# Queries and keys of two strided attention groups by seven half-size products each

## The chip, the cores and the metric

The kernel runs on one core of one Trainium2 chip. The metric is the time of one execution on the device in microseconds (us); the time before is the median of 3 runs.

## The reference

A decoder trunk of two layers over 512 tokens of width 1024, in float32. The first layer mixes tokens by dilated attention, the second by a gated recurrence; each is followed by a convolutional feed-forward network (FFN). The change lies in the attention: 24 heads of width 128 in three groups of eight, with dilations 1, 4 and 16, whose outputs are mixed by their softmax denominators. All queries, keys and values come from one product:

```python
def dilated_attention_mixer(x, w_qkv, w_o, rel_bias):
    qkv = (x @ w_qkv).reshape(B, S, N_GROUPS, 3, HEADS_PER_GROUP, HEAD_DIM)
    for g in range(N_GROUPS):
        o, lse = dilated_group_attention(qkv[:, :, g, 0], qkv[:, :, g, 1], qkv[:, :, g, 2],
                                         tbl, WINDOWS[g], DILATIONS[g])
...
    alpha = jax.nn.softmax(jnp.stack(lses), axis=0)
    o = jnp.sum(alpha[..., None] * jnp.stack(outs), axis=0)
    return o.reshape(B, S, ATTN_OUT_WIDTH).astype(x.dtype) @ w_o
```

## The kernel before, in words

**Precision.** Each float32 factor is cut into a high part and the rest (whi and wlo of a weight, ahi and alo of an activation). A product is three matmuls that add up in a PSUM bank: high by high, high by low, low by high (`PASSES`). The high part is a rounding copy on ACT (L253, half pieces L184), the low part a subtraction on DVE (L265, L185) that waits for it.

**Weights.** All weights stream from HBM in an order written out at the end of the kernel: `plan` lists the loads, `splits` the pieces that are cut from them. `load` issues the loads on SP's queue, with two buffers (`raw`). `pump` cuts the next pieces, if their load has landed by the count of steps (`landed`) and fewer than eight pieces are alive (`W_UNITS`); `tick` runs what is scheduled beside, then calls `pump`. `take` hands a piece to the product that needs it, and cuts it there and then if that has not been done. What `pump` has cut gets its low part later, from `low_parts`, which the next cut or `take` calls. So each engine's instructions stand in the order in which this code emits them, and each engine carries them out in that order.

**Tiles.** `feat_tiles` makes two query or key blocks at a time, one for each head of a pair, each a tile of 24 matmuls of 128x512 (L436) into a bank `ps`. A pair of heads has four such tiles for each of the two strided groups (numbers 1 and 2): queries and keys of both heads. `qk_sink` copies a bank to a tile qk, queries with the scale on ACT (L1181), keys on DVE (L1183). `step` follows each two tiles.

**Beside.** The scores of the pair ahead run as side tasks: products S (L1413), a bias and row sums on DVE (L1294), exponentials on ACT (L1401), weights and transposes on DVE (L1460, L1462), and products O (L1492), copied by ACT (L1495) and added on DVE (L1496).

**Seven for eight.** Values of the local and strided groups, and part of the FFN, are made by seven products of quarters of the matrices instead of eight (`product`, L654, for values; `sevenths`, with 24 matmuls of 128x256 each, L874, for the FFN). They need sums of weight quarters. These are made by transfers on POOL's queue: `add_up` issues a plain load (`first`, L309), and behind it loads that add to what stands there (`sum`, L311). The sums live in one buffer, so the next sum's first load is held until the last low part of the one ahead has been cut: a piece's `behind` entry in `after`, looked up in `finished`. Of two sums, a third is made by an addition on DVE (`mix`, L219). The sums of tokens (T, `token_sums`) are made once for the values. A bank that later products add to is copied by ACT (`kept`, L591).

In the FFN a product of `sevenths` is followed by a plain tile, by its `yield`.

Of the kernel before, what the change touches and what calls it, by code (L numbers as in the profile page):

```python
# [18 lines left out]
P = 128  # L19
# [27 lines left out]
DOWN_AT = (3, 5, 6, 7, 8, 9, 12, 13, 15, 16, 17, 18, 19, 22)  # L47
WIDE_STEPS = (1, 3, 1, 2)
# [47 lines left out]
def kernel(  # L96
# [110 lines left out]
    def split_next(i, j):  # L207
        splits.append((i, j))
        todo[i] += 1
# [204 lines left out]
    def w_seven(w, a, b, beside, before):  # L414

        n = len(plan)
        add("first", 4, 256, [(corner_of(w, 0, b), 256)], before.get("mix"), False)
        add("sum", 4, 256, [(corner_of(w, 0, a), 256)], None, False)
        add("first1", 4, 256, [(corner_of(w, 1, b), 256)], before.get("sum"), False)
        v0 = w_cols(w, beside[0], own=False)  # L420
        left = w_cols(w, a, "halves", False)
        mix = add("mix", 4, 256, [], None, False)
        v1 = w_cols(w, beside[1], own=False)
        last = add("last", 8, 256, [(corner_of(w, 1, b), 4), (corner_of(w, 0, b), 4), (corner_of(w, 1, b), 4)], None, False)
        more = add("sum1", 4, 256, [(corner_of(w, 1, a), 256)], (mix, 1), False)
        for key in (
            (v0, 0), (mix, 0), (v0, 1), (left, 0), (left, 1), (mix, 1), (v1, 0), (last, 0), (v1, 1), (last, 1), (more, 0),
        ):
            split_next(*key)
        before.update(mix=(mix, 0), sum=(more, 0))  # L430
# [232 lines left out]

    def two(s="vq"):
        return [psum(s) for _ in range(2)]
# [172 lines left out]
    def ffn(layer, hT, post, pre, spill):  # L838
# [27 lines left out]
        def sevenths(j, n):  # L866
            outs = {}

            def product(bank, piece, act, first=True):
                W = take(*piece)  # L870
                for n in range(2):
                    for k in range(4):
                        for p, (a, b) in enumerate(PASSES):
                            mm(  # L874
                                bank[:, n * 256 : (n + 1) * 256],
                                W[a][:, k, n * P : (n + 1) * P],
                                woven(act(b)[:, k, :]),
                                start=first and (n, k, p) == (0, 0, 0),
                                stop=(k, p) == (3, 2),
                                skip_group_check=True,  # L880
                            )
                done()

# [13 lines left out]
            product(W, (n + 5, 0), total_of(3))  # L897
            w = kept(W, -1.0)
            yield
            product(X, (n + 4, 0), corner(hT, 0, 0))  # L900
# [3 lines left out]
            product(Z, (n + 4, 1), corner(hT, 1, 0))  # L904
            out(0, 0, c, Z, add)
            yield
            product(X, (n + 5, 1), total_of(2), False)
            u = kept(X, -1.0)
            yield
            product(W, (n + 7, 0), total_of(4), False)  # L910
            out(1, 0, u, W, sub)
            yield
            product(X, (n + 7, 1), total_of(1), False)
# [4 lines left out]
            product(Z, (n + 8, 0), corner(hT, 1, 1))  # L918
# [186 lines left out]
    def attention(hT, post, pre, spill):  # L1105
# [57 lines left out]
        def qk(ps, scale, permute, turned=True, halves=False):  # L1163
# [20 lines left out]
            return o  # L1184

# [375 lines left out]
        for hp in range(4):  # L1561
# [4 lines left out]
            for j in range(4):  # L1566
# [9 lines left out]
                feat_tiles(1, hT, lambda m, ps: sink(2 * j + m, ps), between=held if last and j == 3 else None, paired=False)  # L1576
# [177 lines left out]
    for hp in range(4):  # L1754
        if hp == 0:
            w_value(qkv, (2 * D, 512))
        for j in range(2):
            w_cols(qkv, j * D + hp * 256)
            value_part("l", hp, j)
    for hp in range(4):  # L1760
        for c, (g, j) in enumerate(((1, 0), (1, 1), (2, 0), (2, 1))):
            w_cols(qkv, g * 3 * D + j * D + hp * 256)
            value_part("s", hp, c)
    for c in range(4):
        w_rows(attn_w_o[0], c * 256)
# [122 lines left out]
```

## Time and profile before

| | us |
|---|---|
| median of 3 runs | 1373.49 (1370.64 to 1374.04) |
| the profiled execution | 1373.19 |
| its span, first to last instruction | 1371.2 |
| TensorE busy in it | 1352.8 |
| DVE busy | 1026.3 |
| ACT busy | 692.2 |

The mean clock that TensorE was granted is 0.997 of full. The profile's page gives each engine's busy time and share of the span, the groups of instructions by line with their mean duration in ns, and the transfers by queue. A timeline lists single instructions, with the start and the duration in us, the engine, the line, the operation and its tiles; the bracket is the idle time ahead of it and what ended it. The chain of waits goes back from the last instruction, and has for each piece its start, its length and what it was. PE is TensorE, PEld its weight loads.

### The profile page before, as it was taken

How to read it: one execution, taken by the hardware profiler on the slowest of the kernel's cores; microseconds unless marked ns; L12 is line 12 of the kernel's file. 1: busy time of each engine (PE TensorE's matmuls, PEld its weight loads, DVE VectorE, ACT ScalarE, POOL GpSimd, SP SyncE). 2: the span in 40 equal slices, each digit the busy share in tenths (PEclk: the TensorE clock that was granted, in tenths of full speed). 3: DMA queues.
4: the chain of work that ended last, by engine and by line, in shares of the span. 5: the costliest groups of instructions: out<-in, count | busy, mean ns of one | idle time of the engine just before them, and what ended most of it. 6: DMA issues, size and time to landing. Idle time of an engine off the chain costs nothing.

```text
span 1371.2 us, 18713 instructions
## 1 busy us (share of the span) xinstructions
PE 1352.8 (99%) x7109; PEld 1199.5 (87%) x7109; DVE 1026.3 (75%) x1790; ACT 692.2 (50%) x1169; POOL 111.8 (8%) x126
## 2 busy tenths in 40 slices
PE   9999999999999999999999999999999999999997
PEld 6888888888888889998888889888898998888886
DVE  7787573637667679877958769878979877958765
ACT  5434432414355554455645545579655455645642
POOL 2211021011000001000000010000001000000110
PEclk9999999999999999999999999999999999999999
DMA  8979779596748354555668793233144565768771
GB/s 256 246 223 282 189 189 253 197 218 165 237 152 302 107 170 114 157 175 123 200 175 197 203 270 123 93 123 122 62 148 121 163 185 116 207 170 196 210 192 62
DMA packets 184236, 243.10 MB, mean 177 GB/s; under 512 B 16632, under 2 KB 135936, under 8 KB 184146
## 3 DMA queue, kind: packets, MB, share of 16 engines
q1 hardware_dynamic: 151456, 184.82, 41.1%
q0 software_dynamic: 32688, 57.09, 21.7%
q8 instruction: 56, 0.92, 0.3%
q14 instruction: 34, 0.28, 0.1%
q10 hardware_dynamic: 2, 0.00, 0.0%
HBM read 218.23 MB, written 28.36 MB: 180 GB/s over the span
## 4 chain that ended last, share of the span: by engine, by line
PE 60%; DVE 9%; ACT 4%; issue 2%; DMA 1%; POOL 0%; DVEq 0%; ACTq 0%; POOLq 0%
PE ps L436 35%; PE acc L436 8%; PE X L654 5%; PE vq L654 3%; PE W L654 3%; PE X L874 2%; DVE wlo L265 2%; PE Z L874 2%; PE W L874 2%; DVE xb L1607 1%; DMA sum<-in_attn_w_qkv_dram 1%; PE O L1492 1%; DVE x L551 1%; DVE post L546 1%; DVE th L1662 1%
## 5 line engine op out<-in xcount | busy, mean ns | idle before, releaser
L436 PE MATMUL ps<-hT,whi 128*128 128x512 f32 (+1 forms) x2528 | 697.8, 362 | 0.8 <-DVE hT L499 0.6
L436 PEld LDWEIGHTS ps<-hT,whi 128*128 128x128 f32 x2528 | 459.4, 190 | 57.5 <-issue 1.3
L436 PE MATMUL ps<-hT,wlo 128*128 128x512 f32 (+1 forms) x1264 | 456.1, 361 | 1.5 <-DVE wlo L265 1.5
L265 DVE TENSOR_TENSOR wlo<-raw,whi 128x1024 fp32r<-128x1024 f32 x233 | 280.3, 1218 | 22.9 <-ACT whi L253 22.7
L253 ACT ACTIVATE whi<-raw 128x1024 fp32r<-128x1024 f32 x233 | 239.6, 1052 | 107.0 <-DMA raw<-in_attn_w_qkv_dram 78.2
L436 PEld LDWEIGHTS ps<-hT,wlo 128*128 128x128 f32 x1264 | 239.8, 190 | 29.8 <-DVE wlo L265 1.9
L847 DVE SCALAR_TENSOR_TENSOR u<-ps,cols,u 128x511 f32<-128x511 f32 (+1 forms) x160 | 119.6, 747 | 66.3 <-ACT u L843 63.0
L253 ACT ACTIVATE whi<-sum 128x1024 fp32r<-128x1024 f32 x68 | 70.8, 1051 | 127.2 <-DMA sum<-in_attn_w_qkv_dram 70.9
L265 DVE TENSOR_TENSOR wlo<-sum,whi 128x1024 fp32r<-128x1024 f32 x68 | 82.1, 1219 | 48.5 <-ACT whi L253 48.5
L436 PE MATMUL acc<-whi,ahi 128*128 128x512 f32 x256 | 98.2, 383 | 0.0
L436 PE MATMUL acc<-wlo,ahi 128*128 128x512 f32 x256 | 97.1, 379 | 0.2 <-DVE wlo L265 0.2
L436 PE MATMUL acc<-whi,alo 128*128 128x512 f32 x256 | 97.1, 379 | 0.0
L857 ACT ACTIVATE u<-u 128x512 f32<-128x512 f32 x48 | 30.3, 631 | 99.6 <-DVE u L847 99.6
L843 ACT ACTIVATE u<-ps,cols 128x512 f32<-128x512 f32 x80 | 61.4, 768 | 24.1 <-PE ps L436 24.1
L654 PE MATMUL vq<-whi,T 128*128 128x512 f32 x192 | 59.7, 382 | 0.0
L654 PE MATMUL X<-whi,A 128*128 128x512 f32 x192 | 59.1, 379 | 0.0
L436 PEld LDWEIGHTS acc<-whi,alo 128*128 128x128 f32 x256 | 48.4, 189 | 7.2 <-DVE alo L185 0.4
L436 PEld LDWEIGHTS acc<-wlo,ahi 128*128 128x128 f32 x256 | 48.4, 189 | 7.1 <-DVE wlo L265 0.6
L436 PEld LDWEIGHTS acc<-whi,ahi 128*128 128x128 f32 x256 | 48.4, 189 | 6.7 <-ACT ahi L184 0.2
L311 POOL DMA_DIRECT2D sum<-in_ffn_w_down_dram x16 | 20.6, 1289 | 357.9 <-DMA sum<-in_ffn_w_down_dram 141.0
L859 DVE TENSOR_TENSOR u<-u,u 128x512 f32<-128x512 f32 x48 | 33.2, 693 | 13.2 <-ACT u L857 12.1
L654 PEld LDWEIGHTS X<-whi,A 128*128 128x128 f32 x192 | 36.3, 189 | 5.1
(252 smaller groups left out, 1969.3 us busy)
## 6 DMA issues: line engine op xcount, KB each, us to landing
raw<-in_ffn_w_up_dram SPq DMA_DIRECT2D x44, 1024.0 KB
raw<-in_attn_w_qkv_dram SPq DMA_DIRECT2D x25, 1024.0 KB
raw<-in_ffn_w_down_dram SPq DMA_DIRECT2D x16, 1024.0 KB
sum<-in_ffn_w_down_dram POOLq DMA_DIRECT2D x16, 1024.0 KB, 8.9
sum<-in_attn_w_qkv_dram POOLq DMA_DIRECT2D x24, 512.0 KB, 8.2
raw<-in_attn_w_qkv_dram SPq DMA_DIRECT2D x16, 512.0 KB
sum<-in_ffn_w_down_dram SPq DMA_DIRECT2D x8, 1024.0 KB
raw<-in_lru_w_in_dram SPq DMA_DIRECT2D x8, 1024.0 KB
```

The costliest lines, as they stand in the source:

```text
L253: nc.scalar.activation(hi, raw, AF.Copy)
L265: nc.vector.tensor_tensor(lo, raw, hi.bitcast(F32), op=ALU.subtract)
L311: nc.gpsimd.dma_start(dst, src, accum_op=ALU.add)
L436: mm(dst, l[a], r[b], start=start and n == 0, stop=stop and n == 2)
L546: nc.vector.tensor_tensor(in_two(u[i]), unwoven(banks[i]), in_two(gh[i]), op=ALU.mult)
L551: nc.vector.scalar_tensor_tensor(xh[i], u[i], y, xh[i], op0=ALU.mult, op1=ALU.add)
L654: mm(banks[u], act(a)[:, 2 * j + k, u * P : (u + 1) * P], woven(W[b][:, k, :]), start=first and (j, k, n) == (0, 0, 0), stop=(j, k, n) == ...
L843: nc.scalar.activation(u, ps, AF.Identity, scale=cc[:, j : j + 1], bias=cc[:, 48 + j : 49 + j])
L847: nc.vector.scalar_tensor_tensor(u[:, d:], ps[:, : S - d], wc, u[:, d:], op0=ALU.mult, op1=ALU.add)
L857: nc.scalar.activation(u, u, AF.Gelu_apprx_tanh)
L859: nc.vector.tensor_tensor(gv[k], gv[k], u, op=ALU.mult)
L874: mm(bank[:, n * 256 : (n + 1) * 256], W[a][:, k, n * P : (n + 1) * P], woven(act(b)[:, k, :]), start=first and (n, k, p) == (0, 0, 0), st ...
```

## The change

For two of the eight strided groups of the head pairs, group 2 of the third pair and group 1 of the fourth, the four tiles give way to `crossed`: seven products of 24 matmuls of 128x256 (`corner_product`, L671 of the changed kernel, the FFN's function moved out under a new name). Columns a and b of the weight are the query's and the key's columns of both heads; partial sums stay in the banks W, X and Z. The weights come by `w_seven`, as in the FFN but without plain tiles beside (`beside` is None): a load `first`, accumulating loads `sum`, and `first1`, the DVE addition `mix`, one load of quarters, one that is added to, and `sum1`. The first of these transfers stands behind the last value sum (`chain[-1]`), the next group's behind the sums of the first. Lines of the changed kernel differ by one or two from those of before in the upper half, and by 17 in `product` (L690 for L673) or about 46 (L1506 for L1460, L1340 for L1294, L1447 for L1401) further down; L593 is `kept`, L254 and L266 are high and low parts, L220 is `mix`.

```diff
+CROSSED = [(2, 2), (3, 1)]
...
-        v0 = w_cols(w, beside[0], own=False)
+        v0 = w_cols(w, beside[0], own=False) if beside else None
         left = w_cols(w, a, "halves", False)
         mix = add("mix", 4, 256, [], None, False)
-        v1 = w_cols(w, beside[1], own=False)
+        v1 = w_cols(w, beside[1], own=False) if beside else None
...
         last = add("last", 8, 256, [(corner_of(w, 1, b), 4), (corner_of(w, 0, b), 4), (corner_of(w, 1, b), 4)], None, False)
         more = add("sum1", 4, 256, [(corner_of(w, 1, a), 256)], (mix, 1), False)
         for key in (
             (v0, 0), (mix, 0), (v0, 1), (left, 0), (left, 1), (mix, 1), (v1, 0), (last, 0), (v1, 1), (last, 1), (more, 0),
         ):
-            split_next(*key)
+            if key[0] is not None:
+                split_next(*key)
...
+    def corner_product(bank, piece, act, first=True):
+        W = take(*piece)
+        for n in range(2):
+            for k in range(4):
+                for p, (a, b) in enumerate(PASSES):
+                    mm(
+                        bank[:, n * 256 : (n + 1) * 256],
+                        W[a][:, k, n * P : (n + 1) * P],
+                        woven(act(b)[:, k, :]),
+                        start=first and (n, k, p) == (0, 0, 0),
+                        stop=(k, p) == (3, 2),
+                        skip_group_check=True,
+                    )
+        done()
...
+        def crossed(qs, ks, turned):
+
+            n = state["next"]
+            state["next"] += 7
+            o = [[gen(s="qk") for _ in range(2)] for _ in range(2)]
+            qs.extend(o[0])
+            ks.extend(o[1])
+
+            def out(f, t, op):
+                for h in range(2):
+                    if f and turned:
+                        dst = o[f][h].rearrange("p (m t a k) -> p t m a k", m=16, t=2, a=2)[:, t]
+                        how, sizes = "p (k m a) -> p m a k", dict(m=16, a=2)
+                    else:
+                        dst = o[f][h].rearrange("p (r t a u) -> p t r a u", r=4, t=2, a=2)[:, t]
+                        how, sizes = "p (u r a) -> p r a u", dict(r=4, a=2)
+                    op(dst, lambda x: x[:, h * 256 : (h + 1) * 256].rearrange(how, **sizes))
+
+            tt, stt = nc.vector.tensor_tensor, nc.vector.scalar_tensor_tensor
+            W, X = psum("W"), psum("X")
+            corner_product(W, (n + 4, 0), total_of(3))
+            w = kept(W, -1.0)
+            pump(1)
+            corner_product(X, (n + 3, 0), corner(hT, 0, 0))
+            c = kept(X, SCALE)
+            tick()
+            Z = psum("Z")
+            corner_product(Z, (n + 3, 1), corner(hT, 1, 0))
+            out(0, 0, lambda d, v: stt(d, v(Z), SCALE, v(c), op0=ALU.mult, op1=ALU.add))
+            pump(1)
+            corner_product(X, (n + 4, 1), total_of(2), False)
+            u = kept(X, -1.0)
+            tick()
+            corner_product(W, (n + 5, 0), total_of(4), False)
+            out(1, 0, lambda d, v: tt(d, v(u), v(W), op=ALU.subtract))
+            pump(1)
+            corner_product(X, (n + 5, 1), total_of(1), False)
+            x = kept(X, SCALE)
+            out(1, 1, lambda d, v: tt(d, v(w), v(X), op=ALU.subtract))
+            tick()
+            Z = psum("Z")
+            corner_product(Z, (n + 6, 0), corner(hT, 1, 1))
+            out(0, 1, lambda d, v: stt(d, v(Z), SCALE, v(x), op0=ALU.mult, op1=ALU.add))
...
-                feat_tiles(1, hT, lambda m, ps: sink(2 * j + m, ps), between=held if last and j == 3 else None, paired=False)
+                if (hp, 1 + j // 2) not in CROSSED:
+                    feat_tiles(1, hT, lambda m, ps: sink(2 * j + m, ps), between=held if last and j == 3 else None, paired=False)
+                elif j % 2:
+                    crossed(qs, ks, not last)
+                    tick()
+                    if last and j == 3:
+                        held()
...
+    crossed_after = {}
     for hp in range(4):
         for c, (g, j) in enumerate(((1, 0), (1, 1), (2, 0), (2, 1))):
-            w_cols(qkv, g * 3 * D + j * D + hp * 256)
+            c0 = g * 3 * D + hp * 256
+            if (hp, g) not in CROSSED:
+                w_cols(qkv, c0 + j * D)
+            elif not j:
+                w_seven(qkv, c0, c0 + D, None, crossed_after)
             value_part("s", hp, c)
+            crossed_after.update(dict.fromkeys(("mix", "sum"), chain[-1]) if (hp, c) == (2, 1) else {})
```

How the instructions stand: on DVE, at the end of the value block ahead of the first new group. sum_231 is the buffer of the value sums, wlo a low part, v a value, ps a bank. Before:

```order
L1434 TENSOR_TENSOR s_3047<-st_1970,s_3043 128x4
L265 TENSOR_TENSOR wlo_2975<-sum_231,whi_2974 128x1024
L673 SCALAR_TENSOR_TENSOR v_3091<-y_2608,vq_3065 128x512
L673 SCALAR_TENSOR_TENSOR v_3092<-y_2609,vq_3066 128x512
L1443 TENSOR_TENSOR s_3045<-s_3047,st_1970 128x4
L1446 TENSOR_TENSOR s_3045<-s_3045,s_3018 128x4
L1447 TENSOR_TENSOR s_3045<-s_3045,s_3018 128x4
L1448 RECIPROCAL s_3046<-s_3045 128x4
```

and after:

```order
L1506 TENSOR_TENSOR L_3028<-L_3028,s_3048 128x512
L1508 STREAM_TRANSPOSE LT_3105<-L_3028 128x512
L1506 TENSOR_TENSOR L_3040<-L_3040,s_3048 128x512
L1508 STREAM_TRANSPOSE LT_3108<-L_3040 128x512
L1510 TENSOR_TENSOR s_3049<-s_3049,s_3048 128x4
L1185 COPY qk_3137<-ps_3112 128x512
L1185 COPY qk_3169<-ps_3144 128x512
L266 TENSOR_TENSOR wlo_2977<-sum_231,whi_2976 128x1024
L690 SCALAR_TENSOR_TENSOR y_2608<-y_2608,vq_3179 128x512
```

The low part that is cut from sum_231 stood ahead of the two values v and the softmax (L1460, L1462). It now stands behind the softmax and behind two copies of key banks.

On POOL, between the biases (toe) of that pair and of the next. Before:

```order
L1149 DMA toe_2932<-skew_133 128x128
L1149 DMA toe_2944<-skew_134 128x128
L1149 DMA toe_3019<-skew_133 128x128
L1149 DMA toe_3031<-skew_134 128x128
L1149 DMA toe_3444<-skew_133 128x128
```

and after:

```order
L1151 DMA toe_2934<-skew_133 128x128
L1151 DMA toe_2946<-skew_134 128x128
L1151 DMA toe_3021<-skew_133 128x128
L1151 DMA toe_3033<-skew_134 128x128
L310 DMA sum_3222<-in_attn_w_qkv_dram 128x4x256
L312 DMA sum_3222<-in_attn_w_qkv_dram 128x4x256
L310 DMA sum_3222<-in_attn_w_qkv_dram 128x4x256
```

Three transfers into the new sum's tile, sum_3222, a first one, an adding one and again a first one, stand here in a row; before, there was none after the biases.

On ACT, in the first of the two groups; raw_ tiles are weights, c_ copies of a finished bank. Before:

```order
L253 ACTIVATE whi_3061<-raw_2863 128x1024
L253 ACTIVATE whi_3114<-raw_2863 128x1024
L253 ACTIVATE whi_3118<-raw_2901 128x1024
L253 ACTIVATE whi_3156<-raw_2901 128x1024
L253 ACTIVATE whi_3195<-raw_3122 128x1024
L253 ACTIVATE whi_3243<-raw_3122 128x1024
L253 ACTIVATE whi_3247<-raw_3199 128x1024
L1181 ACTIVATE qk_3278<-ps_3253 128x512
L253 ACTIVATE whi_3280<-raw_3199 128x1024
```

and after:

```order
L185 ACTIVATE whi_3241<-sum_3222 128x512 x2
L593 ACTIVATE c_3271<-W_3238 128x512
L254 ACTIVATE whi_3273<-raw_2863 128x1024
L593 ACTIVATE c_3301<-X_3239 128x512
L254 ACTIVATE whi_3303<-raw_2863 128x1024
L254 ACTIVATE whi_3306<-sum_3222 128x1024
L254 ACTIVATE whi_3339<-raw_2901 128x1024
L593 ACTIVATE c_3370<-X_3239 128x512
L254 ACTIVATE whi_3372<-raw_2901 128x1024
L254 ACTIVATE whi_3376<-sum_3222 128x1024
L593 ACTIVATE c_3434<-X_3239 128x512
```

Seven high parts stood in a row ahead of a query copy (L1181). Now each bank's copy (L593) stands between them, ahead of the high part for a later product.

On ACT, in the second group, after:

```order
L593 ACTIVATE c_3568<-X_3506 128x512
L1485 ACTIVATE s_3600<-s_3600 128x4
L1447 ACTIVATE L_3579,s_3571<-L_3579,s_3597 128x4x32 x4
L1447 ACTIVATE L_3591,s_3571<-L_3591,s_3597 128x4x32 x4
L254 ACTIVATE whi_3614<-raw_3310 128x1024
L254 ACTIVATE whi_3617<-sum_3222 128x1024
L254 ACTIVATE whi_3650<-raw_3380 128x1024
L593 ACTIVATE c_3679<-X_3506 128x512
```

The high part whi_3614 of the third product is behind eight exponentials (L1447), and what is for the fourth and the fifth follows it.

More of the change, by code (lines that the diff above doesn't have):

```diff
@@ L867, in sevenths @@
             outs = {}
[L869 to L882, printed above, removed]
             def out(p, s, a, q=None, op=None):
@@ L896, in sevenths @@
             W, X = psum("W"), psum("X")
-            product(W, (n + 5, 0), total_of(3))
+            corner_product(W, (n + 5, 0), total_of(3))
             w = kept(W, -1.0)
             yield
-            product(X, (n + 4, 0), corner(hT, 0, 0))
+            corner_product(X, (n + 4, 0), corner(hT, 0, 0))
             c = kept(X)
@@ L903, in sevenths @@
             Z = psum("Z")
-            product(Z, (n + 4, 1), corner(hT, 1, 0))
+            corner_product(Z, (n + 4, 1), corner(hT, 1, 0))
             out(0, 0, c, Z, add)
             yield
-            product(X, (n + 5, 1), total_of(2), False)
+            corner_product(X, (n + 5, 1), total_of(2), False)
             u = kept(X, -1.0)
             yield
-            product(W, (n + 7, 0), total_of(4), False)
+            corner_product(W, (n + 7, 0), total_of(4), False)
             out(1, 0, u, W, sub)
             yield
-            product(X, (n + 7, 1), total_of(1), False)
+            corner_product(X, (n + 7, 1), total_of(1), False)
             out(0, 1, X)
@@ L917, in sevenths @@
             Z = psum("Z")
-            product(Z, (n + 8, 0), corner(hT, 1, 1))
+            corner_product(Z, (n + 8, 0), corner(hT, 1, 1))
             out(0, 1, None, Z, add)
```

## The prediction

> **What bounds the kernel now.** I read the page's busy shares first: TensorE is busy 99% of the span, and no other engine over 87%. The two stretches that the change rewrites stand in the chain of waits from 352 to 403 us, so I read that next, then the engines' timelines there. The first two rows below are the page's, the others pieces of the chain (start, length).
>
> ```profile
> PE 1352.8 (99%) x7109; PEld 1199.5 (87%) x7109; DVE 1026.3 (75%) x1790; ACT 692.2 (50%) x1169; POOL 111.8 (8%) x126
> sum<-in_attn_w_qkv_dram POOLq DMA_DIRECT2D x24, 512.0 KB, 8.2
> ...
> 321.29 13.14 DMA sum<-in_attn_w_qkv_dram
> ...
> 353.14 1.15 DVE wlo L265
> ...
> 354.33 15.38 PE ps L436 x70
> 369.70 1.88 PE O L1492 x16
> ...
> 376.76 1.88 PE O L1492 x16
> 378.64 5.18 PE ps L436 x24
> 383.82 1.78 PE S L1413 x16
> ...
> 534.53 2.68 PE W L874 x24
> 537.21 5.18 PE ps L436 x24
> ```
>
> The first of the two groups (the third head pair's second) has its four tiles from 352.2 on, with two rounds of output products (O) between, up to 378.6; the second group's four, with two rounds of scores (S), follow from there. From 354.33 on the chain is TensorE alone: a tile of 24 matmuls takes 5.18 us (last row), one of the seven products 2.68 (the row above it, from the FFN), and what is saved on TensorE is saved. But what must arrive arrives from ACT and DVE, and the second of the next rows shows the one wait that stands here already, for a low part.
>
> ```profile
> 349.85 0.38 PE L654 MATMUL vq<-wlo,T 128*128 128x512 f32 x1
> 352.23 0.59 PE L436 MATMUL ps<-hT,whi 128*128 128x512 f32 x2
> 354.33 0.48 PE L436 MATMUL ps<-hT,wlo 128*128 128x512 f32 x1 [1.50 <-DVE wlo L265]
> ```
>
> Every tile starts like this: two matmuls on high parts, and the third needs the low part.
>
> **The work that goes.** 4 x 5.18 = 20.7 us of tiles become 7 x 2.68 = 18.8 in each group: -2.0 twice, -3.9. With the wait above (352.4 to 354.3, its 1.50 and the gap before it, -1.7 at best) that is all that the change can give back.
>
> **The first product of the first group** waits for a chain that had no part in this place. In before the low part of the last value sum was cut at 346.49, ahead of the value's second half (from about 349.6). In after it stands behind the other head's softmax and two key copies, whose times I take from the same stretch:
>
> ```profile
> 346.49 1.22 DVE L265 TENSOR_TENSOR wlo<-sum,whi 128x1024 fp32r<-128x1024 f32 x1
> 350.34 0.69 DVE L1460 TENSOR_TENSOR L<-L,s 128x512 f32<-128x512 f32 x1
> 353.02 0.12 DVE L1464 TENSOR_TENSOR s<-s,s 128x4 f32<-128x4 f32 x1
> 355.33 0.68 DVE L1183 COPY qk<-ps 128x512 f32<-128x512 f32 x1
> ...
> L219 DVE TENSOR_TENSOR sum<-sum 128x1024 f32<-128x1024 f32 x4 | 4.9, 1222 | 6.6 <-DMA sum<-in_ffn_w_up_dram 6.6
> L265 DVE TENSOR_TENSOR wlo<-raw,whi 128x1024 fp32r<-128x1024 f32 x233 | 280.3, 1218 | 22.9 <-ACT whi L253 22.7
> L185 DVE TENSOR_TENSOR wlo<-raw,whi 128x512 fp32r<-128x512 f32 x10 | 6.4, 686 | 0.3 <-ACT whi L184 0.3
> L184 ACT ACTIVATE whi<-raw 128x512 fp32r<-128x512 f32 x10 | 5.7, 618 | 2.3 <-DMA raw<-in_attn_w_qkv_dram 2.3
> ```
>
> Softmax done at 353.1, two copies at 0.6 from one start to the next, a low part of 1.22: 355.5. Only then is the sum's buffer free, and the first transfer of the new sums is behind it. TensorE has the value's second half left, and so stands from about 349.9, first for this, and then for the sums:
>
> ```profile
> 315.21 1.56 POOL L309 DMA_DIRECT2D sum<-in_attn_w_qkv_dram  x2 [18.13 <-ACT whi L253]
> 321.29 1.29 POOL L311 DMA_DIRECT2D sum<-in_attn_w_qkv_dram  x1 [0.34 <-issue]
> ...
> DMA to landing us min/median/max: 4.0/7.6/13.1
> ```
>
> The last row is of the sums between 300 and 360 us. The plain load: 4.0, the shortest of them (the second row's accumulating one is the 13.14 of the chain). Then 0.34 for POOL to go on, and an accumulating load for which I take the page's 8.2; the third load is issued right behind and should land by then. 355.5 + 4.0 + 0.3 + 8.2 = 368.0; the add of the two sums 1.22, half of the high part 0.62, half of the low 0.69: 370.6. The third product of this stretch was due at 352.2, so **+18.4**. Bounds: 4.0 for both loads takes 4.2 off; 8.2 and 13.1 add 9.1.
>
> **The other products of the first group.** Each needs a new piece, and ACT takes its instructions in order. Where it had four high parts in a row, the copy of a finished bank (kept) now stands between them, so the next high part can't start before the product ahead has ended.
>
> ```profile
> L591 ACT ACTIVATE c<-X 128x512 f32<-128x512 f32 x32 | 17.6, 582 | 3.2 <-PE X L654 3.2
> L253 ACT ACTIVATE whi<-raw 128x1024 fp32r<-128x1024 f32 x233 | 239.6, 1052 | 107.0 <-DMA raw<-in_attn_w_qkv_dram 78.2 <-DMA raw<-in_ffn_w_up_dram 20.7 <-DMA raw<-in_ffn_w_down_dram 6.4
> L893 DVE TENSOR_TENSOR w<-c,X 128x256 f32<-128x256 f32 x8 | 3.7, 523 | 4.6 <-ACT w L891 4.6
> L1495 ACT ACTIVATE oT<-O 128x512 f32<-128x512 f32 x8 | 12.2, 1528 | 6.3 <-PE O L1492 5.4 <-DVE alo L185 1.0
> L1496 DVE TENSOR_TENSOR oT<-oT,ow 128x512 f32<-128x512 f32 x8 | 5.5, 693 | 9.0 <-ACT oT L1495 8.5
> L184 ACT ACTIVATE ahi<-oT 128x512 fp32r<-128x512 f32 x8 | 4.8, 622 | 4.7 <-DVE oT L1496 4.7
> L185 DVE TENSOR_TENSOR alo<-oT,ahi 128x512 fp32r<-128x512 f32 x8 | 5.3, 689 | 8.2 <-ACT ahi L184 8.1
> ```
>
> Second and third product: 0.58 + 1.05 + 1.22 from the end of the one before, less hidden beginnings: 2.8 each. The fourth has its high part, but its low part stands behind two outputs from the third bank: 2 x 0.52 + 1.22 = 2.2. Fifth and sixth find theirs ready. The seventh's low part stands behind the attention output's addition: 1.53 + 0.69 + 1.22 = 3.4. Sum **+11.2**. First group: 18.4 + 11.2 - 2.0 - 1.7 = **+25.9**.
>
> **The second group** begins before anything was split ahead. Its first product: behind the second output's copy 1.53, two high parts of outputs 2 x 0.62, a low part 0.69, then add 1.22 and 0.69: 5.4. Its second as above, 2.8. Then scores stand between, and these rows show what the pieces are behind:
>
> ```profile
> 386.05 0.45 DVE L1294 CUSTOM_DVE_ANT_1 L<-S,toe 128x128 f32<-128x128 f32 x1
> 390.07 1.22 DVE L265 TENSOR_TENSOR wlo<-raw,whi 128x1024 fp32r<-128x1024 f32 x1
> ...
> 390.19 0.20 ACT L1439 ACTIVATE s<-s 128x4 f32<-128x4 f32 x1 [5.37 <-DVE s L1434]
> 393.38 1.04 ACT L253 ACTIVATE whi<-raw 128x1024 fp32r<-128x1024 f32 x1
> ```
>
> The scores on DVE and the exponentials on ACT take from 386.05 until a high part has been cut behind them at 394.42: 8.4. In before other tiles covered that; here the third product needs that very piece. With 0.9 from the start of S to DVE's first score, 8.4, the low part 1.2, less S itself 1.7: 8.8. Fourth: 2.2, as above. Fifth: its low part stands behind the second scores (390.07 - 386.05 = 4.0): 0.9 + 4.0 + 1.2 - 1.7 = 4.4. Sixth: its high part behind the second exponentials, 0.9 + 8.4 + 1.2 from the start of S, by when TensorE has done S and, later by 4.4, the fifth product: 10.5 - 1.7 - 4.4 - 2.7 = 1.7. The seventh none. The tile behind the group: its low part is behind two outputs of the sixth bank and a softmax (350.34 to 353.14, 2.8): 1.0 + 0.4 + 2.8 + 1.2 - 2.7 = 2.7. Sum 5.4 + 2.8 + 8.8 + 2.2 + 4.4 + 1.7 + 2.7 = 28.0, less 2.0: **+26.0**. Both groups: **+52**.
>
> **The clock** was full here in before: behind the 1.50 us wait 70 matmuls took 15.38 us, and at 5.18 for 24 they take 15.1. A row elsewhere prices a longer gap:
>
> ```profile
> 486.31 1.08 PE L489 MATMUL tr<-ident,xs 128*128 128x128 f32 x8 [0.69 <-DVE xs L481]
> 492.69 1.94 PE L489 MATMUL tr<-ident,xs 128*128 128x128 f32 x8 [2.62 <-DVE xs L481]
> ...
> 487.00:492.00 5.00, 3.08 (x28) 2.88 (x26) 4.75 (x17) 2.78 (x8) 0.00 (x0) 1.00 0.22 88
> 492.00:496.00 4.00, 3.31 (x17) 3.34 (x18) 3.58 (x6) 2.10 (x4) 0.00 (x1) 0.57 0.87 282
> ```
>
> Behind a gap of 2.6 us the same eight transposes took 1.94 us and not 1.08, and the granted clock of the 4 us around was 0.57. At 0.57 over 4 us the loss is 4.0 x 0.43 = 1.7 us, and that I take for each gap that draws it. Gaps of 2.6 us and more are ten by the terms above (the 18.4 are two, 5.6 and 13). But most are followed by one product of 2.7 us and the next gap, where a slow clock costs nothing, so I take four of the ten: **+7**; bounds 0 and 10 x 1.7 = 17. The Trainium skill ("TensorE: Matmul & The Clock Gate", "Why this matters for your kernels") asks for no idle gaps over about 3 us between bursts, since one idle window brings half rate back. By that rule six gaps would count, at most some 10 us, an estimate from it, and the trace's gap that lost the clock, 2.6 us, is shorter than its bound.
>
> **What costs nothing.** Five more transfers of 512 KB in each group lie on queues that have room (24 such sums land in 8.2 us in the page's row), once what waits for the first of them is paid above. The FFN's product is only moved out of its function. Outputs on DVE (eight of 256 columns and four copies on ACT, for two copies on each) lie beside products, except where counted; uncovered, they would be 8 x 0.52 = 4.2 per group.
>
> **The rivals.**
> *Faster:* the pieces run ahead as in the FFN, where the same seven products stand without a wait (the 534.53 row), and only work goes: 1373.2 - 3.9 - 1.7 = 1367.6. For it: the slots for eight pieces. Against it: the FFN puts a 5.18 us tile behind each seventh, here sevenths follow sevenths, and ACT's order is fixed as listed. It decides from 2.8 us of cover for a piece. 3%.
> *Only the first chain counts:* pieces are cut during the 18 us that TensorE stands, and later waits vanish: 18.4 - 3.9 - 1.7 = +12.8, 1386. Against it: kept stands ahead of them in the order. 6%.
> *The gate stays shut:* every product of both groups runs at half rate because a gap precedes each. 52 + 14 x 2.7 = 52 + 38: 1463. The 0.57 speaks for some of it; that the wait of 1.50 us lost nothing speaks against. The skill's page has the rule of the gate as cited above; by it only gaps over 3 us shut it. 8%.
> The forecast: 83%.
>
> **How the numbers follow.** The profiled execution took 1373.19 us (span 1371.2), 0.3 under the median of 1373.49, so the sum can stand on either: 1373.2 + 52 + 7 = **1432**. Its own range, from fast loads (-4), no clock loss (-7) and the score waits halved (-8) with short hops hidden in the copies (-9): 1404; with slow loads (+9) and all clock losses (+10): 1451. With the rivals' 1386 and part of 1463 it is 1386 to 1458. A measurement of this kernel tells about 0.3% from no change. Faster by more: 0.03, the first rival; within: 0.01; slower: 0.96.
>
> **What would show it.** In the profile after: 5 to 6 us in the middle of the value product that DVE's low part ends; about 13 us before the third matmul of the first L671 product, behind the sums' transfer; gaps near 2.8 us before the second and third, released by the low part behind ACT's kept; 8 to 9 us before the third product of the second group; from 403 us on a shift of about 50 us and nothing new. Wrong would be: no idle time at those places (first rival), gaps only at the first (second), or sevenths of 5 us each (third). If the sums' transfers land at 13 us or the waits for scores are covered, a term is off and not the mechanism.

## The result and the profile after

The changed kernel takes 1452.75 us in the median (1452.17 to 1453.91, 4 runs), the kernel before 1373.07 on the same chip (1370.64 to 1374.04): a ratio of 1.058, 95% interval 1.0567 to 1.0594. That is 79.7 us more. The profiled execution took 1452.43 us, its span is 1450.7.

The page of the changed kernel: TensorE has 22 us more busy time with less work to do, and the two rows by slices (40 slices of 36 us, tenths) have a hole from the tenth to the thirteenth, in TensorE's busy share and in the granted clock alike.

```profile
PE 1374.8 (95%) x7253; PEld 1221.1 (84%) x7253; DVE 1041.5 (72%) x1812; ACT 700.8 (48%) x1181; POOL 122.3 (8%) x136
...
PE   8999999997466999999999999999999999999997
...
PEclk9999999998687999999999999999999999999999
...
sum<-in_attn_w_qkv_dram POOLq DMA_DIRECT2D x32, 512.0 KB, 7.2
```

TensorE's timeline of the changed kernel, the rows with idle time ahead of them (in brackets: how long, and what ended it). L656 is the value product, L671 one of the seven products.

```profile
358.08 0.80 PE L656 MATMUL vq<-wlo,T 128*128 128x512 f32 x1 [7.80 <-DVE wlo L266]
375.38 0.80 PE L671 MATMUL W<-T,whi 128*128 128x256 f32 x2 [12.26 <-ACT whi L185]
378.74 0.58 PE L671 MATMUL W<-T,wlo 128*128 128x256 f32 x1 [2.56 <-DVE wlo L186]
385.32 0.49 PE L671 MATMUL X<-hT,whi 128*128 128x256 f32 x2 [1.63 <-ACT whi L254]
386.59 0.38 PE L671 MATMUL X<-hT,wlo 128*128 128x256 f32 x1 [0.77 <-DVE wlo L266]
...
445.87 0.79 PE L671 MATMUL Z<-hT,whi 128*128 128x256 f32 x2 [6.57 <-ACT whi L254]
...
463.98 0.38 PE L671 MATMUL W<-T,wlo 128*128 128x256 f32 x1 [3.25 <-DVE wlo L266]
```

The waits stand where the prediction put them: the value product for a low part, the first product for the sums, the second for a high and then a low part, the second group's third for the exponentials (6.57), its fifth for the scores (3.25). The row at 378.74 is the third matmul of the first product, due at 370.6 by the prediction.

I added up, from the start of one matmul to the start of the next, what lies over the usual 0.216 us (512 columns) or 0.11 (256) between 347 and 491.5 us. Waits are 63.0 us (2.3 in the same stretch of before), and 171 matmuls that went at just half rate lost 19.4. With the 3.9 us of work that went: 63.0 - 2.3 + 19.4 - 3.9 = 76.2. By the tiles behind it the stretch ends 76.4 us later than in before. The other 3.5 us gather in five small steps over the rest of the span; I did not follow them.

### The profile page after: what moved, and what is told of

It is laid out like the page before. It is cut to its first block, busy times and chain, and to the rows that moved or that the text cites. A ratio compares the mean times of both kernels' runs of the same rounds, so it can differ in the third digit from the quotient of the medians.

```text
span 1450.7 us, 19063 instructions
## 1 busy us (share of the span) xinstructions
PE 1374.8 (95%) x7253; PEld 1221.1 (84%) x7253; DVE 1041.5 (72%) x1812; ACT 700.8 (48%) x1181; POOL 122.3 (8%) x136
## 4 chain that ended last, share of the span: by engine, by line
PE 51%; DVE 11%; ACT 5%; issue 2%; DMA 2%; SPq 0%; DVEq 0%; ACTq 0%; POOLq 0%
PE ps L438 27%; PE acc L438 7%; PE X L656 4%; PE X L671 3%; PE vq L656 3%; PE W L656 3%; DVE wlo L266 2%; PE Z L671 2%; PE W L671 1%; DVE xb L1659 1%; ACT whi L254 1%; DVE x L553 1%; DVE u L864 1%; ACT L L1447 1%; DVE post L548 1%
## 5 line engine op out<-in xcount | busy, mean ns | idle before, releaser
L438 PE MATMUL ps<-hT,whi 128*128 128x512 f32 (+1 forms) x2400 | 661.2, 362 | 0.8 <-DVE hT L501 0.6
L438 PEld LDWEIGHTS ps<-hT,whi 128*128 128x128 f32 x2400 | 436.7, 190 | 54.6 <-ACT whi L254 1.3
L438 PE MATMUL ps<-hT,wlo 128*128 128x512 f32 (+1 forms) x1200 | 432.9, 361 | 3.4 <-DVE wlo L266 3.4
L266 DVE TENSOR_TENSOR wlo<-raw,whi 128x1024 fp32r<-128x1024 f32 x233 | 280.3, 1218 | 48.8 <-ACT whi L254 48.6
L254 ACT ACTIVATE whi<-raw 128x1024 fp32r<-128x1024 f32 x233 | 238.9, 1050 | 96.3 <-DMA raw<-in_attn_w_qkv_dram 61.3
L438 PEld LDWEIGHTS ps<-hT,wlo 128*128 128x128 f32 x1200 | 228.4, 190 | 30.1 <-DVE wlo L266 3.8
L254 ACT ACTIVATE whi<-sum 128x1024 fp32r<-128x1024 f32 x72 | 75.0, 1052 | 126.6 <-DMA sum<-in_attn_w_qkv_dram 70.7
L266 DVE TENSOR_TENSOR wlo<-sum,whi 128x1024 fp32r<-128x1024 f32 x72 | 87.0, 1218 | 49.6 <-ACT whi L254 49.6
L656 PE MATMUL vq<-whi,T 128*128 128x512 f32 x192 | 61.3, 391 | 0.0
L656 PE MATMUL X<-whi,A 128*128 128x512 f32 x192 | 59.1, 379 | 0.0
L671 PE MATMUL W<-T,whi 128*128 128x256 f32 x192 | 37.8, 300 | 14.9 <-ACT whi L185 14.9
L671 PEld LDWEIGHTS W<-T,whi 128*128 128x128 f32 x192 | 33.5, 214 | 16.2 <-ACT whi L185 15.8
```

Source lines behind the costliest of these rows:

```text
L254: nc.scalar.activation(hi, raw, AF.Copy)
L266: nc.vector.tensor_tensor(lo, raw, hi.bitcast(F32), op=ALU.subtract)
L438: mm(dst, l[a], r[b], start=start and n == 0, stop=stop and n == 2)
L656: mm(banks[u], act(a)[:, 2 * j + k, u * P : (u + 1) * P], woven(W[b][:, k, :]), start=first and (j, k, n) == (0, 0, 0), stop=(j, k, n) == ...
L671: mm(bank[:, n * 256 : (n + 1) * 256], W[a][:, k, n * P : (n + 1) * P], woven(act(b)[:, k, :]), start=first and (n, k, p) == (0, 0, 0), st ...
```

## The experiments

The theory: waits on pieces that the queues of DVE, ACT and POOL deliver late, and behind these waits a clock at half rate. The times below are set beside the kernel before on the same chip: 1371.8 for the first four runs, 1372.2 for the next four, 1373.0 for the ninth and tenth, 1371.5 for the eleventh, 1374.6 for the twelfth. Each variant was run once, but for the two that have a ratio beside them (4 executions each). Line numbers move with the edits: L671, L672, L673 and L676 are the matmul of `corner_product`, L266 and L268 the low part, L593, L595 and L597 `kept`.

### One group at a time

```diff
-CROSSED = [(2, 2), (3, 1)]
+CROSSED = [(2, 2)]
```

> Only the third pair's group goes by seven products; the fourth pair's stays with four tiles. Theory (waits in the order of the queues plus a half-rate clock behind them): the shift that the changed kernel shows up to the end of the first group, 422.6 less 378.4 = 44 us, stays, and the 32 us of the second go: 1373 + 44 = about 1417. Rival (the whole cost is the one chain of the first sums, the second group only drags it along): nearly all of 80 us stays, about 1450.

Measured 1417.88, 46.1 over before. As the theory had it.

```diff
-CROSSED = [(2, 2), (3, 1)]
+CROSSED = [(3, 1)]
```

> Only the fourth pair's group goes by seven products. Theory: its sums have the whole third pair to be made in, so the chain of the first sums costs nothing here, and the waits of this group stay (behind kept, scores and exponentials): the second group's 32 us or a few less, 1398 to 1406. Rival (the chain of the first sums is the cost, wherever the first such group stands): about 26 us more than that, near 1430.

Measured 1388.82, only 17.0 over, less than either said. The two do not add up: 46.1 and 17.0 are 63.1, and together they cost 79.7. Behind the third pair's group the fourth's begins with nothing cut ahead; by itself it begins with its first product ready. ACT's row of this run shows another kind of wait, which comes back below: cut ahead of time, a high part stands waiting for its sum to land, and all of ACT with it.

```profile
366.14 1.06 ACT L254 ACTIVATE whi<-sum 128x1024 fp32r<-128x1024 f32 x1 [13.15 <-DMA sum<-in_attn_w_qkv_dram]
```

### The low part last

In `corner_product`, the 16 matmuls on high parts of the weights first, then the 8 on low parts:

```diff
-        for n in range(2):
-            for k in range(4):
-                for p, (a, b) in enumerate(PASSES):
+        seq = [(n, k, p) for n in range(2) for k in range(4) for p in range(2)]
+        seq += [(n, k, 2) for n in range(2) for k in range(4)]
+        for n, k, p in seq:
+            a, b = PASSES[p]
```

> In each of the seven products the 8 matmuls that need the low part of the weights come after the 16 that do not, so that 1.8 us at full rate and 3.4 at half lie between the high part and the need for the low one. Theory: the waits of the third matmul (22 us over the fourteen products in the changed kernel) lose up to 1.8 each: 15 to 20 us off, 1433 to 1438. Rival (the high part, behind the copy of the bank, is what is late, and the low part comes right behind): 5 us off at most, 1448.

Measured 1435.88, 16.9 less than the changed kernel. TensorE's rows of this run: the wait of the second product for its low part is gone, the one for its high part is the same 1.63.

```profile
383.33 2.05 PE L672 MATMUL X<-hT,whi 128*128 128x256 f32 x16 [1.63 <-ACT whi L254]
387.91 2.05 PE L672 MATMUL Z<-hT,whi 128*128 128x256 f32 x16 [1.63 <-ACT whi L254]
393.23 1.16 PE L672 MATMUL X<-T,wlo 128*128 128x256 f32 x8 [0.59 <-DVE wlo L266]
```

Waits are 54.7 us here, for 63.0, and half-rate matmuls lose 12.5, for 19.4: nearly half of the gain is the clock.

### Filling the gaps

`fill(bank, count)` issues matmuls of 128x512 into the bank that the next product starts, and the product's start discards them:

```diff
+            fills = (55, 10, 10, 12) if not len(filled) else (10, 10, 28, 0)
...
+            fill(W, fills[0])
             corner_product(W, (n + 4, 0), total_of(3))
...
+            fill(X, fills[1])
             corner_product(X, (n + 3, 0), corner(hT, 0, 0))
```

> Matmuls that nobody reads fill most of the gaps ahead of the products that start a bank (55 of 128x512 ahead of the first, 10 to 28 ahead of six others; each is overwritten by the product's own start); nothing else is changed. Theory: the idle gaps are what costs the clock, so the half-rate matmuls (171 of them, 19.4 us lost) mostly go and the waits stay: 13 to 19 us off, 1434 to 1440. Rival (these products run at half rate by themselves, or the gaps have nothing to do with it): no gain, and where the filling lasts longer than the gap a loss: 1452 to 1460.

Measured 1445.39: 7.4 less, half of what the theory expected, and not the rival's loss. The second product, its gap filled, took 2.84 us for 5.4 (0.9 of that a wait for its low part); the products whose wait lies between their second and third matmul, where this filling can't stand, went on at half rate. So it decides against "slow by themselves", and leaves the size open. The last two runs of the study take that up.

### The first sums sooner

The low part of the last value sum is cut when the list of pieces has nothing to cut:

```diff
                 units[i, j] = (hi, lo)
                 state["live"] += 1
+            elif i is not None and i < state["lagging"] and plan[i][0] in ("mix", "halves"):
+                low_parts()
             loads()
```

> The low part of the last value sum is cut as soon as the cutting of weights finds nothing to cut, instead of with the next piece; nothing else differs. Theory: the value product no longer waits 8.2 us, and the first transfer of the new sums goes out at about 348 and not at 358.65, so the first product starts about 10 us sooner: 9 to 12 us off, 1441 to 1444. Rival (the sums land when the transfers and the loads beside them let them, not by the start of the chain): 3 us off at most.

Measured 1420.06: 32.7 less, three times what I expected. The first transfer went out at 350.80, for 358.65, and the first product began at 367.25, for 375.38: that is 8 us. The other 25 I had not seen; by the sums over the stretch, waits fell to 45.7 us and the loss to the clock to 6.6. The list of pieces is worked off in order, and at its head stood the sum. Its transfer waited for that low part, that low part waited for the next cut, and the next cut was the sum. Only the value product, which needs the low part, broke the circle. Until then nothing behind the sum was cut ahead either, and that is why ACT had a bank's copy between each two high parts. With the circle broken ACT cuts seven high parts in a row, as in before, and the second group shows what the change was to bring. The window of the whole second group in this run (columns: busy us of PE, PEld, DVE, ACT, POOL, then clock, DMA share, GB/s):

```profile
416.10:438.80 22.70, 22.65 (x202) 22.46 (x202) 19.61 (x56) 11.04 (x27) 1.50 (x4) 1.00 0.52 147
```

Seven products and two rounds of S in 22.7 us without a wait, and at full clock. Four tiles and the same rounds took 24.4 in before (378.39 to 402.77). So the saving is there, some 1.7 us a group. The first group of this run pays for it, ACT first at one sum and then at the next, with the copies of the banks behind it:

```profile
366.14 1.06 ACT L254 ACTIVATE whi<-sum 128x1024 fp32r<-128x1024 f32 x1 [13.52 <-DMA sum<-in_attn_w_qkv_dram]
...
388.47 1.06 ACT L254 ACTIVATE whi<-sum 128x1024 fp32r<-128x1024 f32 x1 [16.53 <-DMA sum<-in_attn_w_qkv_dram]
389.43 0.58 ACT L595 ACTIVATE c<-W 128x512 f32<-128x512 f32 x1
```

### Pieces cut ahead, and all together

On top of that, the four pieces that need no sum stand first in the list, and the two products that use the first two of them go first:

```diff
-LAGS = {"sum": 2, "rows": 2}
+LAGS = {"sum": 2, "rows": 2, "mix": 9}
...
+            (left, 0), (left, 1), (last, 0), (last, 1), (mix, 0), (mix, 1), (more, 0),
...
+            pump(2)
             W, X = psum("W"), psum("X")
-            corner_product(W, (n + 4, 0), total_of(3))
-            w = kept(W, -1.0)
-            pump(1)
             corner_product(X, (n + 3, 0), corner(hT, 0, 0))
             c = kept(X, SCALE)
-            tick()
+            pump(2)
             Z = psum("Z")
             corner_product(Z, (n + 3, 1), corner(hT, 1, 0))
...
+            tick()
+            corner_product(W, (n + 4, 0), total_of(3))
+            w = kept(W, -1.0)
+            pump(2)
```

> The low part of the last value sum early, as in the run ahead of this one; and the pieces that need no sum (four of seven) are cut ahead of the group, the two products that use the first two of them go first, and the sums' pieces are cut last. Theory: the waits behind kept, scores and exponentials go for those four, and the first sums get 5.4 us of products for cover; of 63 us of waits some 30 stay, with half of the 19 us of clock: 1400 to 1412. Rival (the order on ACT and DVE is not what holds the products; the sums are): no more than the early start gives, and 5 us of cover, 1432 to 1438.

Measured 1409.44, as the theory had it. Then with the low part last, too:

> The run ahead of this one with the matmuls on low parts last in each product, too. Theory: another 8 to 12 us off, since the sums' pieces still wait for their low parts: 1390 to 1402. Rival (what is left is the sums' transfers alone, which this cannot hide): 3 us off at most.

Measured 1409.94: no gain, the rival's case. Both runs wait for the sums at the same two places, the third product of each group, now the first that needs a sum. Here are the rows of the second run (the view ends inside the product of the last row, so that it counts 11 of its 16 matmuls):

```profile
368.87 3.79 PE L676 MATMUL W<-T,whi 128*128 128x256 f32 x16 [9.05 <-ACT whi L185]
377.35 3.55 PE L676 MATMUL X<-T,whi 128*128 128x256 f32 x16 [3.25 <-ACT whi L185]
...
412.51 2.72 PE L676 MATMUL W<-T,whi 128*128 128x256 f32 x11 [8.86 <-ACT whi L185]
```

In the run ahead of it the same matmuls begin at 368.61 and 412.51. What comes sooner in between only waits longer there. The first of the two is the transfers: the first sum's plain load goes out at 349.72, its adding load at 357.14, and the product can't begin before 368.9. The second is again work on DVE and ACT: the sum's addition, at 408.54, and its high part, at 411.85, stand behind a round of scores on DVE and of exponentials on ACT.

### The cheaper group alone, in that order

```diff
-CROSSED = [(2, 2), (3, 1)]
+CROSSED = [(3, 1)]
-LAGS = {"sum": 2, "rows": 2, "mix": 9}
+LAGS = {"sum": 2, "rows": 2, "mix": 3}
```

> Only the fourth pair's group by seven products, with the edits of the run ahead of this one, and with the sums' pieces cut ahead of the group, too, since they have landed by then. Theory: with six of seven pieces ready the waits of this group (17.7 us in the run of the fourth pair's group alone) go to some 4, and the 2.0 us of matmuls that go are to be seen against them: 1373 to 1378. Rival (seven products next to each other leave DVE and ACT too little time, whatever the order): 1383 or more.

Measured 1402.24 (ratio 1.021, 1.0186 to 1.0237): worse than this group alone without the edits (1388.82). The theory fell. I had the second load's pieces cut ahead, and the half of it that POOL adds to had not landed (ACT's row, then TensorE's):

```profile
385.38 1.06 ACT L254 ACTIVATE whi<-raw 128x1024 fp32r<-128x1024 f32 x1 [11.10 <-DMA raw<-in_attn_w_qkv_dram]
...
400.38 2.03 PE L676 MATMUL X<-T,wlo 128*128 128x256 f32 x8 [5.21 <-DVE wlo L268]
```

ACT stands 11.1 us, the scores behind it come later, and the fourth product's low part stands behind the scores.

So I cut each piece only when its transfer should have landed, with the list in the order left, mix, last, more:

```diff
-LAGS = {"sum": 2, "rows": 2, "mix": 9}
+LAGS = {"sum": 2, "rows": 2, "mix": 4, "sum1": 4}
```

> Both groups, with the edits of the run of all together, but a piece is cut ahead only when its transfer has had time to land: the two pieces that need no sum first, the first sums four steps after they were issued, the other load's pieces behind them, the last sum four steps late. Theory (what was left in the runs of the ahead kind is ACT and DVE standing at a transfer, with copies and scores queued behind): the first sums still cost about 15 us, and the rest falls to some 10: 1394 to 1402. Rival (the sums' transfers alone set the pace, whatever stands ahead of them in the queues): 1406 to 1412 as there.

Measured 1431.54, outside of both. Now the pieces behind the sums came too late, the fifth product of the second group above all (427.27, 7.31 us).

```profile
369.74 3.48 PE L676 MATMUL W<-T,whi 128*128 128x256 f32 x16 [9.77 <-ACT whi L254]
...
427.27 3.71 PE L676 MATMUL W<-T,whi 128*128 128x256 f32 x16 [7.31 <-ACT whi L254]
```

And the fourth pair's group alone with `"mix": 3, "sum1": 2`:

> Only the fourth pair's group, in the same manner, with the first sums three steps late. Theory: neither ACT nor DVE stands at a transfer here, the first five products find their pieces, and some 4 to 8 us of waits stay behind the exponentials and ahead of the next tile: 1375 to 1381, still not faster than before. Rival (seven products in a row leave DVE and ACT too little time between scores and softmax): 1386 or more, as in the run of this group alone.

Measured 1388.17 (ratio 1.0105, 1.0085 to 1.0125), the rival's figure. The profiled execution, which took 1391.39, has 17.2 us of waits and 5.5 of clock, where this group without the edits had 17.7 and 3.5. But the rival's cause is not shown, since what the theory asks for did not come about. ACT still stands at a load and at a sum, and the copy of a bank, which TensorE waits for, stands behind them:

```profile
385.09 1.06 ACT L254 ACTIVATE whi<-raw 128x1024 fp32r<-128x1024 f32 x1 [9.11 <-DMA raw<-in_attn_w_qkv_dram]
...
390.13 1.06 ACT L254 ACTIVATE whi<-sum 128x1024 fp32r<-128x1024 f32 x1 [3.00 <-DMA sum<-in_attn_w_qkv_dram]
...
393.70 2.99 PE L676 MATMUL X<-T,whi 128*128 128x256 f32 x16 [3.12 <-ACT c L597]
```

The next wait, 4.17 us ahead of the fifth product, does stand behind exponentials. And in the run with the first sums sooner seven products in a row went without a wait. For this group alone each order that I tried moved the waits and did not lessen their sum; with both groups it fell, from 63.0 to some 32 us in the run with the pieces cut ahead. No version beat the kernel before. Whether one could is open.

### The clock by itself

`zeros` is a tile of 128x128 zeros, so that the filling adds nothing to the product's own bank and can stand inside a product:

```diff
+        def fill(count, start):
+            for _ in range(count):
+                mm(bank, zeros, woven(fill_by[0][0][:, 1, :]), start=start, stop=False, skip_group_check=True)
+
+        fill(fills[0], first)
...
+                    if (n, k, p) == (0, 0, 2):
+                        fill(fills[1], False)
```

> Filling again, now with matmuls by zero weights that add nothing to the product's own bank, so that they can stand inside a product too: ahead of its first matmul and ahead of its third, at each wait that the changed kernel shows in its fourteen products, for some 85% of its length (the wait in the value product and that of the tile behind the second group stay unfilled). Theory: no product of the fourteen runs at half rate any more; of the 19.4 us some 4 stay at the two unfilled places, and the waits themselves stay as they are: 1437 to 1442. Rival (the slow matmuls come from something else, or a wait grows by what the clock gives back): 1448 or more.

Measured 2449.23 us. The page shows why this says nothing of the gaps: the granted clock is 0.556 from the first slice on, when nothing had been filled yet.

```profile
PE 2436.9 (100%) x7439; PEld 1595.5 (65%) x7439; DVE 1047.2 (43%) x1813; ACT 715.6 (29%) x1181; POOL 122.1 (5%) x136
...
PEclk6555555555555555555555555555555555555555
```

One thing differs from the start: `zeros` is a tile of the first pool, and so the buffers behind it lie 512 bytes higher. I moved it to the end:

```diff
-    zeros = cp.tile([P, P], F32R, tag="zeros", name="zeros")
+    zeros = sp.tile([P, P], F32R, tag="zeros", name="zeros", bufs=1)
```

> The run ahead of this one again, with the 512 bytes of zero weights set at the end of the memory and not at its start, so that every other buffer lies where it lay before. There the whole execution went at a granted clock of 0.556, from its first tile on, long before the filling begins. If the shift of the buffers did that: a clock of 0.98 or more here, and the filling then tells what it was made for: without half-rate products 1437 to 1442, else 1448 or more. If the filling or that chip's state did it: 2400 again, or anything between.

Measured 1436.69, at the lower end of the theory's range. The waits are what they were (the first product's first matmul at 374.99, for 375.38), only filled. Windows of the changed kernel, and then of this run, over the first group's products and the second's (the clock is the column after POOL's):

```profile
375.00:404.00 29.00, 19.12 (x91) 17.88 (x92) 8.28 (x9) 5.83 (x8) 2.07 (x2) 0.68 0.26 81
404.00:437.00 33.00, 23.41 (x161) 22.27 (x161) 13.02 (x18) 8.89 (x13) 3.94 (x4) 0.86 0.49 110
```

```profile
375.00:404.00 29.00, 28.01 (x196) 24.81 (x197) 10.77 (x13) 8.64 (x11) 2.38 (x3) 1.00 0.44 125
404.00:437.00 33.00, 28.64 (x181) 24.53 (x179) 15.50 (x36) 12.61 (x29) 4.18 (x5) 1.00 0.33 67
```

From 0.68 and 0.86 to 1.00, with the gaps filled and nothing else changed but the tile of zeros: the half-rate clock is made by the gaps, and is worth 16 us here (spans 1450.7 and 1434.9).

## Why the prediction was right, and where its sizes were off

It forecast 1432 within 1386 to 1458, slower; measured 1452.75. That is 1.8 us above the upper end that its own terms give, 1451; only the part of the third rival's 1463 that it added covers it, so that the number lies inside is in part luck. The mechanism stands: waits took the place of the work. Its sum, 59 us, is 20.7 short of the measured 79.7: 5.4 in the waits, 12.4 in the clock, 3.5 elsewhere in the span, less 0.6 for waits in before that it took too small. By its terms:

**The work that goes**, -2.0 us a group: right, though it shows only where nothing waits (22.7 us for 24.4 in the second group of the run with the first sums sooner, which is 1.7 less).

**The first product**, +18.4: 8.1 more, within its bounds. POOL and DVE show where. The load that is added to (L336) stood ahead of the biases on POOL, which was idle for 15.6 us until it could go, so the scores' bias came late and DVE with it (the first row of DVE below stands at 342.42 in before):

```profile
338.50 1.30 POOL L336 DMA_DIRECT2D raw<-in_attn_w_qkv_dram  x1 [15.60 <-DVE s L1492]
339.25 2.25 POOL L1151 DMA_DIRECT2D toe<-skew  x3
...
358.65 0.76 POOL L310 DMA_DIRECT2D sum<-in_attn_w_qkv_dram  x1 [11.01 <-DVE wlo L266]
365.56 1.32 POOL L312 DMA_DIRECT2D sum<-in_attn_w_qkv_dram  x1 [6.15 <-DMA sum<-in_attn_w_qkv_dram]
```

```profile
344.92 0.47 DVE L1340 CUSTOM_DVE_ANT_1 L<-S,toe 128x128 f32<-128x128 f32 x1 [2.52 <-DMA toe<-skew]
...
376.86 1.22 DVE L220 TENSOR_TENSOR sum<-sum 128x1024 f32<-128x1024 f32 x1 [11.81 <-DMA sum<-in_attn_w_qkv_dram]
```

That is 2.5 us: a queue that I had the order of, and did not count what it was moved past. Then 0.6 to the issue; 6.9 from issue to issue for the plain load, for my 4.3 (+2.6); and 11.3 from the adding load's issue to the addition, for 8.2, since the third load landed last (+3.1). The high part ran beside the addition (-0.7).

**The other waits**: in brackets what was measured, over the usual time from start to start. 2.8 was forecast for the second and third product (2.7 to 2.8, each in two gaps), 2.2 for the fourth (2.3), 3.4 for the seventh (3.0); in the second group 5.4 for the first (2.8 and 1.9), 8.8 for the third (6.7 and 0.8), 4.4 for the fifth (3.4), 1.7 for the sixth (0.7), 2.7 for the tile behind (3.6). All waits together: 18.4 + 11.2 + 28.0 = 57.6 forecast, 63.0 measured. The order of the rows named each of them. What I did not see is that many had one cause, the circle at the head of the list: when the low part was cut sooner, the second group lost its waits altogether, though not one of its own lines had been touched.

**The clock** is the step that was mis-sized: +7, measured 19.4 from the half-rate matmuls, and 16 by filling. I took 1.7 us for one gap and counted four, and supposed that a slow clock between short gaps costs nothing. The 1.7 was about right; there were eleven drops to half rate between 347 and 491.5 us. These rows of the changed kernel, its third product's end and the fourth, show otherwise:

```profile
397.60 0.39 PE L671 MATMUL Z<-hT,whi 128*128 128x256 f32 x2
...
400.44 0.55 PE L671 MATMUL X<-T,wlo 128*128 128x256 f32 x1 [2.13 <-DVE wlo L266]
400.79 0.64 PE L671 MATMUL X<-T,whi 128*128 128x256 f32 x2
...
403.35 0.64 PE L671 MATMUL X<-T,whi 128*128 128x256 f32 x2
...
403.96 0.39 PE L671 MATMUL X<-T,whi 128*128 128x256 f32 x2
```

Two matmuls take 0.39 us at full rate and 0.64 behind a gap of 2.13, up to about 403.9: 3.4 us at half rate. With a gap behind each product 150 of the 336 matmuls of the fourteen went slow. And that a slow clock costs nothing where a gap follows was wrong, because the gap hangs on the product's end: the copy of the bank waits for it, and a later end moves the next wait along whole: the gap ahead of the third product is 1.63 us here and in the run with the low part last, where the product ahead of it goes at full rate. The Trainium skill ("TensorE: Matmul & The Clock Gate", "Why this matters for your kernels") sets the bound of harmless gaps at about 3 us. The trace disagrees: 2.13 us were enough here, and so were 1.63 ahead of the second product with 0.77 inside it. In the run of the third pair's group alone the same place has a gap of 1.93, and the clock is slow ahead of it and full behind it:

```profile
397.17 0.64 PE L671 MATMUL X<-T,whi 128*128 128x256 f32 x2
399.74 0.38 PE L671 MATMUL X<-T,wlo 128*128 128x256 f32 x1 [1.93 <-DVE wlo L266]
399.95 0.39 PE L671 MATMUL X<-T,whi 128*128 128x256 f32 x2
```

So it is not the length of a gap that decides. The trace records each change of the granted clock, and these changes all lie on a grid of 3.413 us. Here are four stretches of that grid in the changed kernel (length, then TensorE's busy us; the clock is the column behind POOL's):

```profile
397.14:400.55 3.41, 1.28 (x12) 1.09 (x10) 2.42 (x4) 0.00 (x0) 0.00 (x0) 0.99 0.30 101
400.55:403.97 3.42, 3.42 (x17) 3.42 (x18) 0.98 (x1) 0.00 (x0) 2.07 (x2) 0.51 0.30 37
410.79:414.21 3.42, 1.73 (x15) 1.54 (x14) 2.43 (x5) 1.38 (x2) 1.38 (x2) 1.00 1.03 223
414.21:417.62 3.41, 2.25 (x20) 2.25 (x21) 1.10 (x1) 0.00 (x0) 1.86 (x3) 1.00 1.07 156
```

The gap of 2.13 lies inside the first stretch, TensorE is busy for 1.28 us of it, and the next stretch goes at half rate. The gap ahead of the seventh product's third matmul (415.37) is longer, 2.85 us, but an edge of the grid cuts it in two, each side is busy for half or more (1.73 and 2.25), and the clock stays full. The 1.93 us of the other run are cut in the same way. In thirteen traces of this case (all but the one at 0.556; without the first 20 and the last 10 us of each) it holds throughout: of the stretches at full rate, all 63 with TensorE busy for less than 40% are followed by half rate, none of the 5060 with more than 50%, and 9 of the 13 between. Back to full rate it goes behind 71 of 74 half-rate stretches with more than 80%, and behind 1 of 52 with less. The rival by which every product goes at half rate (1463) was right for nearly half of their matmuls.

**The rivals** "faster" and "only the first chain counts" fell with the rows at 385.32, 445.87 and 463.98.

## What to carry to other kernels

A group of products made cheaper by 2 us is worth that only if its operands come as fast as before: count for each new piece what stands ahead of it on every engine's queue, and look for a list that is worked off in order with a head that waits for the next cut. Price TensorE's gaps twice, as the wait and as the slow clock behind it: in these traces half rate followed a stretch of 3.4 us in which TensorE was busy for less than about half, whatever the single gap, and short products with gaps of 2 us between them are enough for that. When an operand must be made by a chain of transfers, start the chain ahead of all the cover it needs, here some 20 us, or leave the product as it was.

## What the runs showed of the hardware that I had not expected

Buffers that lay 512 bytes higher went with a granted clock of 0.556 over a whole execution, matmuls of 512 columns starting 0.40 us apart for 0.216, and 2449 us; with the same instructions and the buffers in their old places it was 0.993 and 1437. The 0.40 us is neither full rate nor the 0.43 us of the half rate behind gaps. The kernel before took 1371.46 us beside the slow run, on the same chip. Each of the two was run once, so the place may be the cause, and no run shows that it is. The granted clock went by the busy share of fixed stretches of 3.413 us, as above: a gap of 2.13 us was followed by 3.4 us at half rate, one of 2.85 us by none.
